# The last two of 32 experts in a one-core MoE block: order of the x1 loads, of one transpose, of the row scatters, and the branch behind them

## The chip, the core and the metric

The kernel runs on one core of one Trainium2 chip. The core has a matmul engine (TensorE, PE in the profile), a vector engine (VectorE, DVE), a scalar engine (ScalarE, ACT), a general-purpose engine (GpSimd, POOL) and a sequencer without arithmetic (SyncE, SP). Transfers between HBM and on-chip memory are issued from the queues of SP, ACT and POOL. The metric is the device time of one execution in microseconds (us), lower is better; 0.3% of it is 4.8 us.

## What is computed

One layer of a diffusion trunk: attention, gated linear attention and neighbourhood attention on 1024 tokens of width D = 1024, then a mixture of 32 experts in which every token goes to two experts, then a final RMS norm. Only the end of it matters here:

```python
f = hier_moe(h2.reshape(-1, D), w_rg, b_rg, w_re, b_re, w_up, w_down)
x = x + mod[:, 5] * f.reshape(B_, S, D)
...
return rms_norm(x, final_g)
```

An expert takes the rows of its tokens, multiplies them by `w_up` (1024x1024), applies `silu(g) * u` to the two halves, multiplies by `w_down` (512x1024), and its result, times the token's gate, is added to the token's row.

## The kernel before, in words

Each expert has one block of 128 slots (CAP); tokens beyond that go to overflow blocks. `gidx` holds the token of every slot. Experts 0 to 29 (ME = E - HOLD = 30 of them) run in the main loop: POOL gathers the rows, PE multiplies in three passes of rounded pieces, ACT scales the result by the gate, and POOL scatters it with an add into the HBM tensor YS (`y_scatter`, line 1882). The weights come as 128x1024 fp32 tiles (512 KB) through a ring of 34 tiles in SBUF (`ring`, `load_tile`, line 1909 for the issue).

The last two experts, 30 (ME) and 31 (E - 1), are **held**: they run in plain fp32 matmuls, and their results do not go through YS. Beside them the kernel finishes the output. For each of the 8 token tiles t, `pre(t)` (lines 2080 to 2088) multiplies YS's tile by the modulation row m5 on DVE (2082), adds it to the tile of x1, the stream before the experts (2083), writes the sum to the HBM tensor XP from ACT's queue (2084), and squares it on ACT with a row sum (2088). After all eight, `load_rows` (1968) gathers from XP the rows of the tokens that the held experts own, on POOL's queue. `norm` (2131) turns row sums into reciprocal square roots by a chain of eleven small DVE instructions; `scaled` (2135) multiplies a tile by it and by final_g on DVE; `store(t)` (2139) writes it to out from SP's queue. `result(e)` (2118, 2119) scales a held expert's result; it is added to the gathered rows, `cross` adds on PE and DVE the contribution of the first held expert to rows that both own, and `store_rows(i)` (2143) scatters the finished rows of expert ME + i over the output, from POOL's queue.

**What sets the order.** The held part stands in a manual schedule for PE, DVE, ACT and POOL: these run in the order of the program. SP is not in that list; its order is the scheduler's. The loads of the held part come from the list `wants`, one taken each time a tile of the ring comes free: eight x1 tiles (`load_x1`, line 1935), final_g, a tile without a load, the eight YS tiles (`load_y`, line 75 in the profile, a helper) and another tile without a load. A YS load waits for the last `y_scatter`, since YS is tracked in HBM. The first ten are taken in the main loop's last ten steps, the YS loads in `up(ME)`, one for each of its eight tiles. `after_all` makes a row scatter wait for every store and scatter to out before it, so the second row scatter waits for the first.

`up(e)` and `down(e)` are the held experts' two products on PE (line 1994), `hidden(e)` is silu on ACT and the product on DVE (1868, 1869), `turn_hidden(e)` transposes it on PE and copies it on ACT (1988, 1989). In the order before, `turn_hidden(E - 1)` and its ACT copy stand behind `pre(6)` and `pre(7)` and behind `down(ME)`.

Behind the held part stands a loop with as many turns as the register `again` says (line 2190 loads it on all five engines, 2191 is the loop). It is 1 when overflow blocks exist and 0 otherwise; with these inputs it is 0, and the loop's body, which handles overflow and writes the whole output again, is skipped.

Of the kernel before, what the change touches and what calls it, by code (L numbers as in the profile page):

```python
# [8 lines left out]
F32 = mybir.dt.float32  # L9
F32R = mybir.dt.float32r  # L10
I32 = mybir.dt.int32
# [7 lines left out]
D = 1024  # L19
# [46 lines left out]
def body(nc, tc, d, tap=None, upto=None):  # L66
# [7 lines left out]
    def dmab(t, src):  # L74
        nc.sync.dma_start(t, src)
# [1228 lines left out]
    class Til:  # L1304
# [5 lines left out]
        def small(self, name, shape, bufs=2):  # L1310
            return w2.tile([128] + shape, F32, name=name, bufs=bufs)
# [615 lines left out]
    def kept():  # L1927

        x2 = ring()
        rws.pop()  # L1930
        return x2

    def load_x1(t, eng):
        x2 = kept()
        eng.dma_start(x2, X1[t * 128:(t + 1) * 128, :])
        xts.append(x2)

    def small(name, shape):
        return e1.tile([128] + shape, F32, name=name)
# [2 lines left out]
    bs = small("bs", [NOV])  # L1942
    tk, dtk, both = small("tk", [HOLD]), small("dtk", [128]), small("both", [128])
    ones = small("ones", [128])

    def gate_of(e):
        return gxs[e % 6][:, e:e + 1]
# [11 lines left out]
    def held_both():  # L1959

        pt = pe.tile([128, 4, 128], F32, name="ept")
        nc.tensor.matmul(pt[:, 0, :], lhsT=ones, rhs=dtk, start=True, stop=True)
        V.tensor_scalar(both, pt[:, 0, :], tk[:, 0:1], None, op0=OP.is_equal)

    def load_rows(i):

# [5 lines left out]
    def load_y(t):  # L1972
        yts[t] = ring()
        dmab(yts[t], YS[t * 128:(t + 1) * 128, :])

    def load_fg():
        fgs.append(kept())
        dmab(fgs[0], bcast_rows(d["final_g"], D))

    ygs = []  # L1980
    wants = [lambda t=t: load_x1(t, nc.sync) for t in range(NT)] + [load_fg, lambda: ygs.append(kept())]
    wants += [lambda t=t: load_y(t) for t in range(NT)] + [lambda: ygs.append(kept())]

    def turn32(src, n, dst, g):
# [10 lines left out]

    yts, outs = {}, []

    def after_all(i_):

        for o_ in outs:  # L2000
            tc.add_manual_dep(i_.ins, o_.ins.name, mybir.DependencyInfo(mybir.DependencyClass.Sync, mybir.DependencyReason.DATA))

    with tc.manual_schedule(engines={ET.PE, ET.DVE, ET.Activation, ET.Pool}):
        e_gather(gU01[:, 0:1], xgs[0])
# [75 lines left out]
        def pre(t):  # L2080

            V.tensor_mul(yts[t], yts[t], m5)
            V.tensor_add(xts[t], xts[t], yts[t])
            nc.scalar.dma_start(XP[t * 128:(t + 1) * 128, :], xts[t])
            square(t)
# [4 lines left out]
        def up(e, ks):  # L2090
            if ks[0] == 0:
                pu[e] = pe.tile([128, D], F32, name="epu")
            for k in ks:
                mm32(pu[e], k, 8, loaded.pop(NM + 8 * (e - ME) + k), xs[e])
                fill()

        def hidden(e):
            sgs[e] = e_silu(pu[e])

        def turn_hidden(e):  # L2100
            if e == ME:
                a32[ME], a32[E - 1] = (a.bitcast(F32) for a in a_tiles())
            turn32(sgs[e], 4, a32[e], 0)

        def down(e):
            pys[e] = (pd.tile([128, D], F32, name="epy"), pe.tile([128, D], F32, name="epu"))[0] if e == ME else \
                pe.tile([128, D], F32, name="epu")
            for k in range(4):
                mm32(pys[e], k, 4, loaded.pop(NM + 8 * HOLD + 4 * (e - ME) + k), a32[e])
                fill()  # L2110

# [29 lines left out]
        def store_rows(i):  # L2141
            scaled(NT + i)
            i_ = nc.gpsimd.indirect_dma_start(out=d["out"], in_=xts[NT + i], in_offset=None,  # L2143
                                              out_offset=bass.IndirectOffsetOnAxis(ap=gU[:, ME + i:ME + i + 1], axis=0),
                                              bounds_check=T - 1, oob_is_err=False)
            after_all(i_)
            outs.append(i_)


        held_both()  # L2150
        up(ME, range(8))
        pre(0)
        pre(1)
# [5 lines left out]
        pre(4)  # L2159
        pre(5)  # L2160
        hidden(E - 1)
        pre(6)
        pre(7)
        for i in range(HOLD):
            load_rows(i)
        down(ME)
        turn_hidden(E - 1)
        down(E - 1)
        norm(0, 8)
        store(0)  # L2170
        store(1)
        store(2)
        result(ME)
        store(3)
        store(4)
        store(5)
        store(6)
        store(7)
        V.tensor_add(xts[NT], xts[NT], ygd[0])
        square(NT)  # L2180
        cross()
        result(E - 1)
        V.tensor_add(xts[NT + 1], xts[NT + 1], ygd[1])
        square(NT + 1)
        norm(NT, NT + HOLD)
        store_rows(0)
        store_rows(1)


    again = nc.values_load(novt[0:1, 1:2], min_val=0, max_val=1)  # L2190
    with tc.For_i(0, again, 1):
        for e in range(ME, E):
            y_scatter(ygs[e - ME], gU[:, e:e + 1])
        nov = nc.values_load(novt[0:1, 0:1], min_val=0, max_val=NOV)
        with tc.For_i(0, nov, 1) as i:
            ev = nc.values_load(bexp[0:1, ds(i, 1)], engines=[mybir.EngineType.SP], min_val=0, max_val=E - 1)
            gcol = e2.tile([128, 1], I32, name="gcol")
            gsel = e2.tile([128, 2, E], F32, name="gsel", bufs=1)
            g_ = e2.tile([128, 1], F32, name="g_")
            nc.vector.tensor_copy(gcol, gido[:, ds(i, 1)])  # L2200
            e_gather(gcol.bitcast(U32), xgs[0])
            gate_rows(gcol.bitcast(U32), gxs[0])
            nc.vector.tensor_copy(g_, bs[:, ds(i, 1)])
            nc.vector.tensor_scalar(gsel[:, 0, :], cio[:, :E], g_, None, op0=OP.is_equal)
            nc.vector.tensor_mul(gsel[:, 1, :], gsel[:, 0, :], gxs[0])
            nc.vector.tensor_reduce(g_, gsel[:, 1, :], axis=AX.X, op=OP.add)
            x, act = x_tiles(), a_tiles()
            for g in range(2):
                e_turn(xgs[0], 8, *x, g)
            pu_ = pe.tile([128, D], F32, name="epu")  # L2210
            for k, w in enumerate(e_load(d["w_up"][ds(ev, 1)].rearrange("o (k p) f -> p (o k) f", p=128), 8)):
                e_mm(pu_, k, 8, split(w), x)
            e_turn(e_silu(pu_), 4, *act, 0)
            py = pd.tile([128, D], F32, name="epy")
            for k, w in enumerate(e_load(d["w_down"][ds(ev, 1)].rearrange("o (k p) f -> p (o k) f", p=128), 4)):
                e_mm(py, k, 4, split(w), act)
            e_scatter(py, gcol.bitcast(U32), g_)
        for t in range(NT):
            xt, y0 = ring(), ring()
            dmab(xt, X1[t * 128:(t + 1) * 128, :])  # L2220
            dmab(y0, YS[t * 128:(t + 1) * 128, :])
            V.tensor_mul(y0, y0, m5)
            V.tensor_add(xt, xt, y0)
            nc.scalar.activation(y0, xt, AF.Square, accum_out=s3[:, t:t + 1])
            norm(t, t + 1)
            V.scalar_tensor_tensor(xt, xt, r3[:, 0, t:t + 1], fgs[0], op0=OP.mult, op1=OP.mult)
            after_all(nc.sync.dma_start(d["out"][t * 128:(t + 1) * 128, :], xt))
# [127 lines left out]
```

## Time and profile before

| | us |
|---|---|
| Median of three runs | 1604.22 (1602.19 to 1607.95) |
| The profiled execution, its own time | 1601.4 |
| Its span, first to last instruction | 1599.6 |

| Engine | Busy share of the span | Instructions |
|---|---|---|
| PE (matmul) | 91% | 8577 |
| DVE | 71% | 1882 |
| ACT | 60% | 1544 |
| POOL | 29% | 604 |

How to read it: the shares are means over the whole span, and the change lies in its last 95 us, from about 1505 us on. There the page's 40 slices (40 us each) say little; the views that count are the timeline by engine, the waits, and windows of a few us. A row of the timeline gives start, length, engine, line, operation, out<-in, count and, in brackets, the engine's idle time before it and what ended that. The transfers that an engine's queue issues stand under SPq, ACTq and POOL.

### The profile page before, as it was taken

The numbers are of one execution on the slowest core, as the hardware profiler recorded it, in microseconds if no ns is written. First come the engines' busy times: TensorE is split into PE (matmuls) and PEld (weight loads), VectorE is DVE, ScalarE is ACT, GpSimd is POOL, SyncE is SP. The second block draws the span as 40 slices with busy tenths as digits, with TensorE's granted clock in tenths as the row PEclk, the third lists the DMA queues.
The fourth block names the chain that finished last, engine by engine and source line by source line (L and its number), as shares of the span: only waits on it lengthen the run. The fifth ranks groups of instructions, "written<-read, shape, count | busy, mean of one in ns | idle before, by whom it ended". The sixth has DMA issues, their size and how long they took to land. (4 is left out here: it accounts for less than half of the span.)

```text
span 1599.6 us, 24460 instructions
## 1 busy us (share of the span) xinstructions
PE 1449.4 (91%) x8577; PEld 1183.7 (74%) x8577; DVE 1133.4 (71%) x1882; ACT 957.6 (60%) x1544; POOL 463.4 (29%) x604
## 2 busy tenths in 40 slices
PE   6899799889989997899999969999999999999972
PEld 3699577767767766789998857877877888788731
DVE  6612655894544455777777678999999999899755
ACT  3523554773534341677666437887888888888621
POOL 0001433222323211257887552221221122211101
PEclk8999899999988999899999979999999999999996
DMA  9533563014554389412222878999999999999963
GB/s 331 179 103 107 166 223 121 21 48 158 124 129 105 87 278 316 142 49 91 67 82 78 299 270 316 364 363 349 342 368 371 360 362 358 367 349 362 361 257 137
DMA packets 165119, 358.34 MB, mean 224 GB/s; under 512 B 29269, under 2 KB 85056, under 8 KB 164864
## 3 DMA queue, kind: packets, MB, share of 16 engines
q1 hardware_dynamic: 138656, 309.88, 54.6%
q0 software_dynamic: 22880, 36.80, 8.8%
q10 hardware_dynamic: 3456, 10.06, 1.6%
q8 instruction: 68, 1.11, 0.3%
q14 instruction: 59, 0.48, 0.1%
HBM read 319.87 MB, written 57.82 MB: 236 GB/s over the span
## 5 line engine op out<-in xcount | busy, mean ns | idle before, releaser
L1837 DVE TENSOR_TENSOR wlo<-wraw,whi 128x1024 fp32r<-128x1024 f32 x360 | 434.1, 1222 | 53.5 <-ACT whi L1836 48.1
L1836 ACT CAST whi<-wraw 128x1024 fp32r<-128x1024 f32 x360 | 372.5, 1050 | 99.7 <-PE epu L1864 59.0
L1862 PE MATMUL epu<-whi,xh 128*128 128x512 f32 x480 | 195.3, 407 | 2.2 <-ACT xh L1854 2.2
L1863 PE MATMUL epu<-wlo,xh 128*128 128x512 f32 x480 | 194.4, 405 | 0.4 <-DVE wlo L1837 0.4
L1864 PE MATMUL epu<-whi,xl 128*128 128x512 f32 x480 | 191.7, 399 | 0.6 <-DVE xl L1855 0.6
L1268 DVE TENSOR_REDUCE nm<-S 128x1 f32<-128x1280 f32 x64 | 94.9, 1489 | 51.6 <-PE S L1267 42.0
L1841 POOL DMA_INDIRECT xg<-H,gidx x30 | 31.9, 1064 | 342.0 <-PE ept L1852 341.5
L375 PE MATMUL pj<-wh,hh 128*128 128x256 f32 (+1 forms) x384 | 113.8, 296 | 3.1 <-ACT kbT L331 3.1
L1863 PEld LDWEIGHTS epu<-wlo,xh 128*128 128x128 f32 x480 | 91.4, 191 | 29.3 <-DVE wlo L1837 10.4
L377 PE MATMUL pj<-wh,hl 128*128 128x256 f32 (+1 forms) x384 | 112.4, 293 | 0.0
L376 PE MATMUL pj<-wl,hh 128*128 128x256 f32 (+1 forms) x384 | 112.4, 293 | 0.0
L1862 PEld LDWEIGHTS epu<-whi,xh 128*128 128x128 f32 x480 | 91.5, 191 | 22.7 <-ACT xh L1854 2.7
L1864 PEld LDWEIGHTS epu<-whi,xl 128*128 128x128 f32 x480 | 91.2, 190 | 21.8 <-DVE xl L1855 1.3
L1862 PE MATMUL epy<-whi,ah 128*128 128x512 f32 x240 | 100.9, 421 | 2.4 <-ACT y L1888 2.4
L364 PE MATMUL pj<-hh,wh 128*128 128x512 f32 (+1 forms) x240 | 99.8, 416 | 0.0
L1273 ACT ACTIVATE p<-S,nm 128x1280 f32<-128x1280 f32 x64 | 84.6, 1331 | 21.8 <-DMA x1t<-w_out 16.4
L1864 PE MATMUL epy<-whi,al 128*128 128x512 f32 x240 | 95.6, 398 | 0.0
L1863 PE MATMUL epy<-wlo,ah 128*128 128x512 f32 x240 | 95.1, 396 | 0.0
L366 PE MATMUL pj<-hh,wl 128*128 128x512 f32 (+1 forms) x240 | 92.1, 384 | 0.0
L365 PE MATMUL pj<-hl,wh 128*128 128x512 f32 (+1 forms) x240 | 91.9, 383 | 0.0
L1266 PE MATMUL S<-ak,aq 128*128 128x512 f32 (+1 forms) x192 | 75.3, 392 | 12.1 <-ACT p L1273 11.3
L1288 ACT COPY eT<-apt 128x512 f32<-128x512 f32 (+1 forms) x96 | 46.4, 515 | 63.8 <-PE apt L1287 61.9
(485 smaller groups left out, 3476.3 us busy)
## 6 DMA issues: line engine op xcount, KB each, us to landing
wraw<-w_up SPq DMA_DIRECT2D x254, 512.0 KB
wraw<-w_down SPq DMA_DIRECT2D x127, 512.0 KB
wm<-w_mod SPq DMA_DIRECT2D x32, 512.0 KB
raw<-w_in SPq DMA_DIRECT2D x22, 512.0 KB
wm<-w_mod SPq DMA_DIRECT2D x32, 256.0 KB
aq<-QS SPq DMA_DIRECT2D x64, 128.0 KB
ak<-KS SPq DMA_DIRECT2D x8, 640.0 KB
xn<-x SPq DMA_DIRECT2D x8, 512.0 KB
```

Of the source, the lines that this page charges most:

```text
L364: nc.tensor.matmul(ps[:, :n], lhsT=a, rhs=x, start=(k == 0), stop=False)
L365: nc.tensor.matmul(ps[:, :n], lhsT=a, rhs=y, start=False, stop=False)
L366: nc.tensor.matmul(ps[:, :n], lhsT=b, rhs=x, start=False, stop=(k == 7))
L375: nc.tensor.matmul(ps[:, :n], lhsT=a, rhs=wh[:, k, :], start=(k == 0), stop=False)
L376: nc.tensor.matmul(ps[:, :n], lhsT=a, rhs=wl[:, k, :], start=False, stop=False)
L377: nc.tensor.matmul(ps[:, :n], lhsT=b, rhs=wh[:, k, :], start=False, stop=(k == 7))
L1268: V.tensor_reduce(u.nm[:, m:m + 1], sv, axis=AX.X, op=OP.max, negate=True)
L1836: nc.scalar.copy(hi, raw)
L1837: nc.vector.tensor_sub(lo, raw, hi.bitcast(F32))
L1862: nc.tensor.matmul(ps[:, cs], lhsT=ah[:, k, :], rhs=hi[:, cs], start=(k == 0), stop=False)
L1863: nc.tensor.matmul(ps[:, cs], lhsT=ah[:, k, :], rhs=lo[:, cs], start=False, stop=False)
L1864: nc.tensor.matmul(ps[:, cs], lhsT=al[:, k, :], rhs=hi[:, cs], start=False, stop=(k == nk - 1))
```

## The change

- The x1 loads of tiles 2 to 7 are no longer issued when their tile of the ring comes free (`room_x1` only keeps the tile) but in `load_y`: x1 tile t + 2 behind YS tile t.
- `turn_hidden(E - 1)` moves from behind `pre(7)` and `down(ME)` to the middle of `down(ME)`, and `down(ME)` and this transpose move ahead of `pre(6)` and `pre(7)`.
- `held_both` gets five small DVE instructions that build `own`: for a token that both held experts own, the first expert's row index is pushed out of bounds, so that its row is written by the second scatter alone. The scatters use `own`, and each waits for the eight stores only, not for the other scatter.
- In the last part, `result(ME)`, the addition and the square of the first row tile stand after four stores, not eight; the norm of the two row tiles becomes two norms; and the first row scatter is issued before `cross` and `result(E - 1)`.
- `again` is loaded into the engines' registers at the start of the held part, and the last loop becomes a conditional on it.

```diff
@@ -1930,10 +1930,13 @@
         rws.pop()
         return x2
 
-    def load_x1(t, eng):
-        x2 = kept()
-        eng.dma_start(x2, X1[t * 128:(t + 1) * 128, :])
-        xts.append(x2)
+    def load_x1(t):
+        nc.sync.dma_start(xts[t], X1[t * 128:(t + 1) * 128, :])
+
+    def room_x1(t):
+        xts.append(kept())
+        if t < 2:
+            load_x1(t)
 
     def small(name, shape):
         return e1.tile([128] + shape, F32, name=name)
@@ -1942,6 +1945,8 @@
     bs = small("bs", [NOV])
     tk, dtk, both = small("tk", [HOLD]), small("dtk", [128]), small("both", [128])
     ones = small("ones", [128])
+    again2 = small("again2", [1])
+    own = e1.tile([128, HOLD], I32, name="own")
 
     def gate_of(e):
         return gxs[e % 6][:, e:e + 1]
@@ -1961,6 +1966,11 @@
         pt = pe.tile([128, 4, 128], F32, name="ept")
         nc.tensor.matmul(pt[:, 0, :], lhsT=ones, rhs=dtk, start=True, stop=True)
         V.tensor_scalar(both, pt[:, 0, :], tk[:, 0:1], None, op0=OP.is_equal)
+        V.tensor_reduce(again2, both, axis=AX.X, op=OP.max)
+        V.tensor_scalar(again2, again2, 8192.0, None, op0=OP.mult)
+        V.tensor_add(again2, again2, tk[:, 0:1])
+        V.tensor_copy(own[:, 0:1], again2)
+        V.tensor_copy(own[:, 1:2], gidx[:, E - 1:E])
 
     def load_rows(i):
 
@@ -1972,13 +1982,15 @@
     def load_y(t):
         yts[t] = ring()
         dmab(yts[t], YS[t * 128:(t + 1) * 128, :])
+        if t + 2 < NT:
+            load_x1(t + 2)
 
     def load_fg():
         fgs.append(kept())
         dmab(fgs[0], bcast_rows(d["final_g"], D))
 
     ygs = []
-    wants = [lambda t=t: load_x1(t, nc.sync) for t in range(NT)] + [load_fg, lambda: ygs.append(kept())]
+    wants = [lambda t=t: room_x1(t) for t in range(NT)] + [load_fg, lambda: ygs.append(kept())]
     wants += [lambda t=t: load_y(t) for t in range(NT)] + [lambda: ygs.append(kept())]
 
     def turn32(src, n, dst, g):
@@ -1995,10 +2007,12 @@
 
     yts, outs = {}, []
 
+    FULL = mybir.DependencyInfo(mybir.DependencyClass.Sync, mybir.DependencyReason.DATA)
+
     def after_all(i_):
 
         for o_ in outs:
-            tc.add_manual_dep(i_.ins, o_.ins.name, mybir.DependencyInfo(mybir.DependencyClass.Sync, mybir.DependencyReason.DATA))
+            tc.add_manual_dep(i_.ins, o_.ins.name, FULL)
 
     with tc.manual_schedule(engines={ET.PE, ET.DVE, ET.Activation, ET.Pool}):
         e_gather(gU01[:, 0:1], xgs[0])
@@ -2102,10 +2116,10 @@
                 a32[ME], a32[E - 1] = (a.bitcast(F32) for a in a_tiles())
             turn32(sgs[e], 4, a32[e], 0)
 
-        def down(e):
-            pys[e] = (pd.tile([128, D], F32, name="epy"), pe.tile([128, D], F32, name="epu"))[0] if e == ME else \
-                pe.tile([128, D], F32, name="epu")
-            for k in range(4):
+        def down(e, ks=range(4)):
+            if ks[0] == 0:
+                pys[e] = pd.tile([128, D], F32, name="epy") if e == ME else pe.tile([128, D], F32, name="epu")
+            for k in ks:
                 mm32(pys[e], k, 4, loaded.pop(NM + 8 * HOLD + 4 * (e - ME) + k), a32[e])
                 fill()
 
@@ -2141,13 +2155,15 @@
         def store_rows(i):
             scaled(NT + i)
             i_ = nc.gpsimd.indirect_dma_start(out=d["out"], in_=xts[NT + i], in_offset=None,
-                                              out_offset=bass.IndirectOffsetOnAxis(ap=gU[:, ME + i:ME + i + 1], axis=0),
+                                              out_offset=bass.IndirectOffsetOnAxis(ap=own.bitcast(U32)[:, i:i + 1], axis=0),
                                               bounds_check=T - 1, oob_is_err=False)
-            after_all(i_)
+            for o_ in outs[:NT]:
+                tc.add_manual_dep(i_.ins, o_.ins.name, FULL)
             outs.append(i_)
 
 
         held_both()
+        again = nc.values_load(novt[0:1, 1:2], min_val=0, max_val=1)
         up(ME, range(8))
         pre(0)
         pre(1)
@@ -2159,36 +2175,34 @@
         pre(4)
         pre(5)
         hidden(E - 1)
+        down(ME, range(2))
+        turn_hidden(E - 1)
+        down(ME, range(2, 4))
         pre(6)
         pre(7)
         for i in range(HOLD):
             load_rows(i)
-        down(ME)
-        turn_hidden(E - 1)
         down(E - 1)
-        norm(0, 8)
-        store(0)
-        store(1)
-        store(2)
+        norm(0, NT)
+        for t in range(4):
+            store(t)
         result(ME)
-        store(3)
-        store(4)
-        store(5)
-        store(6)
-        store(7)
         V.tensor_add(xts[NT], xts[NT], ygd[0])
         square(NT)
+        for t in range(4, 7):
+            store(t)
+        norm(NT, NT + 1)
+        store(7)
+        store_rows(0)
         cross()
         result(E - 1)
         V.tensor_add(xts[NT + 1], xts[NT + 1], ygd[1])
         square(NT + 1)
-        norm(NT, NT + HOLD)
-        store_rows(0)
+        norm(NT + 1, NT + 2)
         store_rows(1)
 
 
-    again = nc.values_load(novt[0:1, 1:2], min_val=0, max_val=1)
-    with tc.For_i(0, again, 1):
+    with tc.If(again > 0):
         for e in range(ME, E):
             y_scatter(ygs[e - ME], gU[:, e:e + 1])
         nov = nc.values_load(novt[0:1, 0:1], min_val=0, max_val=NOV)
```

## Rows read from the trace of the kernel before

**Rows 1.** Chain of waits in order of time: start us, us, what.

```profile
1582.51 1.80 DMA out<-wraw,gidx
1584.31 3.49 issue
...
1588.39 0.62 POOL out L2143
```

**Rows 2.** Timeline of DVE and PE in the held part.

```profile
1532.98 1.23 DVE L2082 TENSOR_TENSOR wraw<-wraw,m 128x1024 f32<-128x1024 f32 x1 [15.83 <-DMA wraw<-YS]
...
1552.32 0.69 DVE L1869 TENSOR_TENSOR sg<-sg,epu 128x512 f32<-128x512 f32 x1 [2.07 <-ACT sg L1868]
...
1556.58 1.22 DVE L2083 TENSOR_TENSOR wraw<-wraw 128x1024 f32<-128x1024 f32 x1
...
1559.88 10.13 PE L1994 MATMUL epu<-wraw,al 128*128 128x512 f32 x16 [6.16 <-ACT al L1989]
...
1561.62 3.68 DVE L2135 SCALAR_TENSOR_TENSOR wraw<-wraw,r 128x1024 f32<-128x1024 f32 x3
...
1572.51 1.22 DVE L2179 TENSOR_TENSOR wraw<-wraw,wlo 128x1024 f32<-128x1024 f32 x1
...
1578.78 0.17 DVE L2131 TENSOR_SCALAR s<-s 128x2 f32<-128x2 f32 x1 [1.27 <-ACTq L2191]
...
1580.94 2.48 DVE L2135 SCALAR_TENSOR_TENSOR wraw<-wraw,r 128x1024 f32<-128x1024 f32 x2
```

**Rows 3.** Timeline of SP's queue from 1505 us on.

```profile
1506.48 11.61 SPq L1935 DMA_DIRECT2D wraw<-X  x8
1519.05 0.33 SPq L75 DMA_DIRECT2D wraw<-final_g  x1
1526.26 8.25 SPq L75 DMA_DIRECT2D wraw<-YS  x8
1562.93 10.02 SPq L2139 DMA_DIRECT2D out<-wraw  x8
```

**Rows 4.** Timeline of POOL from 1500 us on.

```profile
1517.17 1.55 POOL L1882 DMA_INDIRECT YS<-y,gidx  x1 [8.33 <-DVE both L1963]
1561.56 1.07 POOL L1968 DMA_INDIRECT wraw<-XP,gidx  x1 [42.84 <-issue]
...
1582.51 1.80 POOL L2143 DMA_INDIRECT out<-wraw,gidx  x1 [17.53 <-DVE wraw L2135]
1588.02 0.99 POOL L2143 DMA_INDIRECT out<-wraw,gidx  x1 [3.71 <-issue]
```

**Rows 5.** Lines 1882, 1968 and 2143, one row each: us from issue to landing.

```profile
DMA to landing us min/median/max: 6.7/9.1/10.5
...
DMA to landing us min/median/max: 4.8/6.6/8.3
...
DMA to landing us min/median/max: 3.2/4.0/4.7
```

**Rows 6.** Windows: length, busy us per engine (instructions), PEclk, DMA share, GB/s.

```profile
1522.00:1528.00 6.00, 6.00 (x16) 2.65 (x15) 0.00 (x0) 0.00 (x0) 0.00 (x0) 1.00 0.60 184
1528.00:1541.00 13.00, 13.00 (x32) 5.79 (x31) 5.82 (x6) 2.79 (x5) 0.00 (x0) 1.00 1.01 383
1559.00:1560.20 1.20, 0.32 (x1) 0.32 (x2) 0.68 (x4) 0.83 (x3) 0.00 (x0) 0.50 0.76 311
1560.20:1563.00 2.80, 2.80 (x4) 1.19 (x4) 2.56 (x9) 0.00 (x0) 1.14 (x2) 0.50 0.00 0
```

**Rows 7.** Lines 2190, 2191 and 2351: duration ns min/median/max, first and last start.

```profile
L2190 SPq TENSOR_LOAD <-novt x1: 480/480/480, 1534.6 to 1534.6; - x1
...
L2190 PEldq TENSOR_LOAD <-novt x1: 1507/1507/1507, 1566.9 to 1566.9; - x1
...
L2191 POOLq INC_SWDGE_SEM  x1: 1750/1750/1750, 1588.9 to 1588.9; - x1
...
L2351 POOLq DRAIN  x3: 46/103/6404, 1592.3 to 1599.3; - x3
```

## Prediction, made before the changed kernel was run

> **What bounds it now.** Read the chain of waits first, since it tells which end counts [rows 1]: the last pieces are the transfer of a row scatter into out, 3.5 us in which POOL waits, and the other row scatter. So the end is set by POOL's second scatter. POOL's timeline [rows 4] says why it is so late: the first is issued at 1582.51, the second at 1588.02, though both were scaled by 1583.42 (1580.94 + 2.48) [rows 2]. The gap is the wait for the first to land, between 3.2 and 4.7 us [rows 5].
>
> Next, DVE's timeline [rows 2]. From 1532.98 to 1583.42 DVE hardly rests; before that it idles 15.83 us, and what ends the idling is the first YS tile. SP's timeline shows the cause of that [rows 3]: the eight x1 loads go out from 1506.48 on, final_g at 1519.05, and the YS loads only at 1526.26, since they wait for the last scatter into YS, issued at 1517.17 [rows 4]. The first YS tile then needs another 6.7 us, behind x1 tiles still under way. The windows [rows 6] show the transfer engines at 0.60 of their time from 1522 to 1528, and full, at 383 GB/s, from 1528 to 1541. So the tail has three limits in a row: the scatter into YS with what queues around it, then DVE's list, then POOL's two scatters.
>
> PE is not among them: the last held product starts at 1559.88 after a 6.16 us wait and takes 10.13 us at the low clock (granted 0.50, that is 1.2 GHz [rows 6]), and DVE reaches its result only after 1572.51 [rows 2].
>
> **Part by part**, against the profiled execution (span 1599.6, own time 1601.4, which is 2.8 below the median 1604.22; I take the difference off the median).
>
> *x1 loads behind the YS loads.* Six transfers leave the queue ahead of the scatter and final_g. Scatters into YS land 6.7 to 10.5 us after issue, median 9.1 [rows 5], nearly all beside weight loads. I take 6.7, since the queues would then be nearly free: landing at 1517.17 + 6.7 = 1523.9 instead of about 1526.2. The bounds are 4.7, the worst of the scatters into out, which do not add, and 9.1. The Trainium skill (DMA: Bandwidth & Descriptors, Anatomy of one DMA) gives a transfer issued by GpSimd about 2.0 us plus its bytes over 436 GB/s, some 3.2 us for 512 KB as an estimate; the scatters into out agree (3.2 to 4.7), those into YS do not (6.7 and up), and by that price the forecast would be 3.5 us lower.
>
> How long a lone load takes is bounded by an XP write: pre(7)'s addition ends at 1557.80 and its write, issued behind it, is moved by 1560.2, after which no byte moves [rows 2, 6], so 2.4 us or less; the upper bound is the 6.7 us seen. I take 2.9, near the free one: the first YS tile is there at 1526.8 and DVE starts 6 us earlier.
>
> It cannot keep those 6 us. A tile of 524 kB at 383 GB/s [rows 6] takes 1.37 us. The queue is now y0, x1(2), y1, x1(3), ..., and y5 is its eleventh load; four XP writes will have come between. So y5 is there 10 + 4 = 14 transfers after y0: 1526.8 + 19.2 = 1546.0. pre(5) takes 1.23 + 1.22, then DVE waits 2.07 for silu and multiplies for 0.69 (as at 1552.32), then come pre(6) and pre(7), 4.9 us [rows 2]: 1546.0 + 2.45 + 2.8 + 4.9 = 1556.1, against 1557.80. y7, 19 transfers after y0, is there at 1552.8, in time. **Gain 1.7 us**; the rest of the 6 has gone into the transfer engines.
>
> *Last transpose moved forward.* Its ACT copy no longer stands behind two squares, so PE starts the last product about 6 us sooner, probably at the high clock. Nothing late waits for it: cost and gain 0, covered by DVE's list. Its place in `down(ME)` makes PE wait for DVE's product in mid-way; `result(ME)` wants that output some 8 us later.
>
> *Reordered end.* From 1557.80 to 1583.42 DVE needed 25.6 us; the same instructions remain, and one chain for the norm is added, 1580.94 - 1578.78 = 2.16 us. The gathered rows are wanted sooner. Before, DVE reached their addition 3.82 us (to 1561.62) plus 10.89 us after pre(7); with four stores of 1.23 us fewer ahead it is 9.8 us. The first gather is issued 3.76 us after pre(7) and lands 4.8 to 8.3 us later [rows 2, 4, 5], so 8.6 to 12.1: a wait of 0 to 2.3 us. I take 0.5, since only a few stores compete by then. Together 25.6 + 2.2 + 0.5 = 28.3: the last row is scaled at 1584.4.
>
> *Independent scatters.* The second scatter is issued about 0.3 us after its row is scaled (the first was ready at 1582.18 and began at 1582.51): 1584.7 instead of 1588.02, **gain 3.3 us for all parts so far**. The first goes out some 7 us before it and waits only for eight stores. Landing took 3.2 us for one scatter and 4.7 for the other; I take 4.0, so 0.8 is lost.
>
> *Building own.* Five small DVE instructions of 0.2 to 0.4 us at about 1517, within DVE's 15.83 us of idling: 0. Were that cover gone, some 1.5 us.
>
> *Register loads moved, conditional for loop.* A load took 0.48 us on SP and 1.51 on PE [rows 7]. On PE it now stands ahead of `up(ME)` and shifts both up products by 1.5 us; behind it all PE work of the held part waits, but silu of expert 31 waits for the square of pre(5) anyway. On SP it stands near the YS loads, which wait for the scatter then: 0. Whether the conditional closes faster than a loop without a turn the trace cannot show. POOL's 1.75 us for its counter ran while the scatter was landing, and could come after it; the 6.4 us drain of POOL behind it all [rows 7] could at best go. Bounds: 6.4 us less, 1.75 more. I take 0, as POOL has the same transfers to settle.
>
> Sum: -3.3 + 0.8 = -2.5 us, a span of 1597.1 and a median of about **1601.7 us**. Its own range is 1598 to 1605: landing in 4.7 gives 2 more, in 9.1 takes 2.4; the gather takes up to 1.8; a tile at 1.3 us gives 1.
>
> **Rivals.**
>
> 1. *The order does not come out as written.* SP is left to the scheduler, and the trace has it out of program order: the register load of line 2190, written behind everything, runs on SP at 1534.6 [rows 7], ahead of the eight stores from 1562.93 on [rows 3]. x1 tiles wait for nothing by then, YS tiles do, so x1 may be put first again. Against it: in the same trace the register load, ready long before, was not put ahead of the YS loads. Then DVE starts at 1532.98 as before, pre(7) ends at 1557.80, the second scatter goes at 1557.80 + 28.3 + 0.3 = 1586.4, gain 1.6 less 0.8: **1603.4**.
>
> 2. *The queues are freer than I think*: the scatter lands in 4.7 us and the XP writes give way to the loads. y0 is there at 1524.8, DVE is the limit (24.8 us from 1532.98 to 1557.80), pre(7) ends at 1549.6, and without a wait for the gather the second scatter goes at 1549.6 + 27.8 + 0.3 = 1577.7, 10.3 sooner: **1594.7**. Against it: full engines from 1528 to 1541. The skill's 3.2 us would make it 1.5 us less.
>
> 3. *Slower: the moved loads collide.* The place is the wait of pre(5) for y5; the price six more transfers, 8.2 us, in the stretch that is full already. If the scatter lands no sooner and y0 again takes 6.7 us, it is there at 1532.9 as before, y5 at 1552.1, pre(7) ends at 1562.2, and with a gather wait of 2.3 the second scatter goes at 1592.6: 4.6 later, 5.4 with the landing: **1609.6**. It decides from the point at which y5 lands after 1548.5: then pre(7) ends after 1558.6, which uses up what the scatters gain. For it: 0.60 of the engines' time from 1522 to 1528, left unused by x1 then.
>
> **Numbers.** Forecast 0.50, rival 1 0.23, rival 2 0.13, rival 3 0.14. The range 1595.5 to 1607.5 leaves out about half of rivals 2 and 3. About 0.3% (4.8 us) is what a measurement of this kernel can tell from no change. Faster by more, under 1599.4: three in ten of the forecast, a little of rival 1, all but a little of rival 2, with the unknown of the closing: 0.33. Slower, over 1609.0: over half of rival 3, little else: 0.09. The rest, 0.58, is within.
>
> **What would show it.** Right: on SP the x1 loads stand between YS loads; the scatter into YS lands in under 7 us; DVE's idling ends at about 1527, but DVE waits again, for YS tiles, between pre(3) and pre(5); the two scatters are issued some 7 us apart, without a wait between them; the last one at about 1584.7; POOL's drain of 6.4 us is still there. Wrong: eight x1 loads in one run ahead of final_g (rival 1); no second wait of DVE (rival 2); pre(7) ending after 1558.6 (rival 3); or a drain of another length.

## The result and the profile after

The changed kernel takes 1596.02 us (median of 14 runs, 1585.59 to 1601.54), the kernel before beside it 1604.59 us (14 runs, 1595.54 to 1612.22): a ratio of 0.9941, 95% interval 0.9918 to 0.9964. It is faster by 0.6%. A second measurement on another occasion gave 0.9956 (0.9934 to 0.9979). Two executions in this study, of 4853.16 and 2037.62 us, are left out of every ratio as slow ones.

The profiled execution of the changed kernel took 1598.41 us, with a span of 1596.6 us. That is only 3.0 us less than the span before. The reason is in work that the change leaves alone: the last scatter into YS, the end of the main loop, was issued at 1517.17 before and at 1521.03 after. In the profiled executions of all kernels of this study it lies anywhere between 1509.15 and 1523.53. So a single span says little about an edit of a few us. What can be compared is the **tail**, from the issue of this last scatter (called T0 from here on) to the end of the span: 1599.6 - 1517.17 = 82.4 us before, 1596.6 - 1521.03 = 75.6 us after, 6.9 us less. A repeat of both kernels gave 82.8 and 75.7. These 6.9 of 1604 us are 0.43%, a ratio of 0.9957, which both intervals contain.

The chain of waits of the changed kernel (start us, us, what), to be read against [rows 1]:

```profile
1581.35 1.61 DMA out<-wraw,own
1582.95 3.84 issue
1586.79 0.05 POOLq L2205
...
1587.03 1.00 POOL out L2157
```

POOLq is POOL's sequencer, which hands out the instructions and waits on semaphores. The chain looks like the old one: a row scatter's transfer, an issue gap of 3.8 us, the other scatter. This reading is wrong here, as DVE's timeline shows (columns as in [rows 2]):

```profile
1532.23 1.22 DVE L2096 TENSOR_TENSOR wraw<-wraw,m 128x1024 f32<-128x1024 f32 x1 [10.27 <-DMA wraw<-YS]
...
1535.69 1.23 DVE L2096 TENSOR_TENSOR wraw<-wraw,m 128x1024 f32<-128x1024 f32 x1 [0.98 <-DMA wraw<-YS]
...
1546.45 1.22 DVE L2096 TENSOR_TENSOR wraw<-wraw,m 128x1024 f32<-128x1024 f32 x1 [0.68 <-DMA wraw<-YS]
...
1557.83 1.23 DVE L2097 TENSOR_TENSOR wraw<-wraw 128x1024 f32<-128x1024 f32 x1
...
1569.10 1.23 DVE L2190 TENSOR_TENSOR wraw<-wraw,wlo 128x1024 f32<-128x1024 f32 x1
...
1575.82 2.47 DVE L2149 SCALAR_TENSOR_TENSOR wraw<-wraw,r 128x1024 f32<-128x1024 f32 x2
...
1585.46 1.28 DVE L2149 SCALAR_TENSOR_TENSOR wraw<-wraw,r 128x1024 f32<-128x1024 f32 x1
```

The last row tile is scaled at 1585.46 + 1.28 = 1586.74, and the second scatter goes at 1587.03, 0.29 us behind it. DVE's list now sets the end of this stretch. The two short waits, 0.98 and 0.68 us for YS tiles, are new.

POOL's timeline (for [rows 4]):

```profile
1521.03 1.55 POOL L1882 DMA_INDIRECT YS<-y,gidx  x1 [8.34 <-DVE both L1968]
1562.89 1.07 POOL L1978 DMA_INDIRECT wraw<-XP,gidx  x1 [40.32 <-issue]
...
1581.35 1.61 POOL L2157 DMA_INDIRECT out<-wraw,own  x1 [15.11 <-DVE wlo L2132]
1587.03 1.00 POOL L2157 DMA_INDIRECT out<-wraw,own  x1 [4.08 <-DVEq L2205]
```

SP's timeline (for [rows 3]) shows that the order came out as written, two x1 tiles ahead and the others between the YS tiles:

```profile
1510.97 1.60 SPq L1934 DMA_DIRECT2D wraw<-X  x2
1513.51 0.33 SPq L75 DMA_DIRECT2D wraw<-final_g  x1
1528.45 0.33 SPq L75 DMA_DIRECT2D wraw<-YS  x1
1528.82 0.42 SPq L1934 DMA_DIRECT2D wraw<-X  x1
1529.35 0.38 SPq L75 DMA_DIRECT2D wraw<-YS  x1
1529.77 0.43 SPq L1934 DMA_DIRECT2D wraw<-X  x1
```

The windows (columns as in [rows 6]) show the price and the use of the emptier stretch. From 1522 to 1528 little but the scatter into YS is under way; of the 0.38 MB moved, 0.11 MB are what is left of the earlier loads:

```profile
1522.00:1528.00 6.00, 6.00 (x16) 2.65 (x15) 0.00 (x0) 0.00 (x0) 0.57 (x1) 1.00 0.36 64
1528.00:1541.00 13.00, 13.00 (x32) 5.77 (x31) 5.60 (x6) 2.78 (x5) 0.00 (x0) 1.00 0.89 310
1541.00:1547.00 6.00, 6.00 (x17) 2.65 (x16) 5.25 (x5) 0.00 (x0) 0.00 (x0) 1.00 1.02 417
```

Last, the lines of the conditional and of the closing on POOL, and of the register load (duration ns min/median/max, first and last start, for [rows 7]):

```profile
L2205 POOLq EVENT_SEMAPHORE  x3: 17/43/43, 1587.3 to 1587.5; - x3
...
L2205 POOLq INC_SWDGE_SEM  x1: 1759/1759/1759, 1587.6 to 1587.6; - x1
...
L2365 POOLq DRAIN  x3: 46/103/6402, 1589.4 to 1596.3; - x3
...
L2166 PEldq TENSOR_LOAD <-novt x1: 494/494/494, 1516.0 to 1516.0; - x1
```

The 6.4 us drain is unchanged. It begins as soon as the 1.76 us for POOL's counter is over (1587.6 + 1.76), 2.33 us behind the scatter's issue; before it began at 1592.35 - 1588.02 = 4.33 us behind it [rows 4, 7].

**Where the 6.9 us come from.** The tail is cut into three stretches at two marks, the end of the last y + x1 unit (pre(7), DVE line 2083 before, 2097 after) and the issue of the second row scatter. All times in us, from the timelines:

| | before | after | gain |
|---|---|---|---|
| T0 to the end of pre(7) | 1557.80 - 1517.17 = 40.63 | 1559.06 - 1521.03 = 38.03 | 2.60 |
| pre(7) to the second scatter | 1588.02 - 1557.80 = 30.22 | 1587.03 - 1559.06 = 27.97 | 2.25 |
| second scatter to the end | 1599.6 - 1588.02 = 11.58 | 1596.6 - 1587.03 = 9.57 | 2.01 |

### The profile page after: what moved, and what is told of

Its sections match the earlier page's. It is cut to its first block, busy times and chain, and to the rows that moved or that the text cites. A ratio compares the mean times of both kernels' runs of the same rounds, so it can differ in the third digit from the quotient of the medians.

```text
span 1596.6 us, 24416 instructions
## 1 busy us (share of the span) xinstructions
PE 1448.2 (91%) x8577; PEld 1182.3 (74%) x8577; DVE 1136.5 (71%) x1898; ACT 957.7 (60%) x1544; POOL 462.2 (29%) x604
## 3 DMA queue, kind: packets, MB, share of 16 engines
q8 instruction: 68, 1.11, 0.3%
## 5 line engine op out<-in xcount | busy, mean ns | idle before, releaser
L1268 DVE TENSOR_REDUCE nm<-S 128x1 f32<-128x1280 f32 x64 | 94.9, 1489 | 51.1 <-PE S L1267 41.4
```

What stands on the lines that cost most here:

```text
L1268: V.tensor_reduce(u.nm[:, m:m + 1], sv, axis=AX.X, op=OP.max, negate=True)
```

## The experiments

Each kernel below is read by these three stretches of its profiled execution. Single device times are not used, for those of one kernel vary by 6 us or more either way; where a ratio is given, it comes from 11 or 12 runs.

**Both kernels again.** No edit. They show how far the stretches of the same kernel agree.

> The kernel before once more, for the spread of one look. Measured is the tail, from the issue of the last scatter into YS to the end of the span; it was 82.4 us before (1517.17 to 1599.6) and is 75.6 us after the change (1521.03 to 1596.6). Theory A (the whole gain lies in the tail, and the start of the tail merely scatters from run to run): tail 82.4 within 1 us, and its start anywhere from 1512 to 1524. Rival B (the change also shifted the work ahead of the tail): the start is near 1517.2 again, and one of the changed kernel near 1521.

> The changed kernel once more. Theory A: tail 75.6 within 1 us, start of the tail anywhere from 1512 to 1524, and over the rounds 0.3 to 0.6% faster than before, since 6.9 us is 0.43%. Rival B: start near 1521 again, or a ratio beyond 0.8%, which the tail could not give.

Measured: before 41.0 + 30.3 + 11.6 = 82.8 us, after 38.2 + 28.0 + 9.6 = 75.7 us, ratio 0.9956 (0.9934 to 0.9979). The second and third stretch repeat within 0.1 us, and a difference of 0.2 us in them can be read. The first repeats within 0.4 here, but it varies more than that: the seven profiles of this study with two x1 loads early have 37.2 to 39.1 us (mean 38.1), the four with all eight early 40.3 to 41.0 (mean 40.6). In one profile, less than about 2 us in the first stretch, and so in the tail, can't be laid to an edit.

**The loop back in place of the conditional**, in the changed kernel; the registers are still loaded early.

```diff
-    with tc.If(again > 0):
+    with tc.For_i(0, again, 1):
```

> The changed kernel with the loop in place of the conditional, the register still loaded early. Theory A: the loop's closing waits for the landing of the last scatter before POOL's drain of 6.4 us may start, the conditional's does not; from the issue of the last row scatter to the start of the drain 4.3 us as before the change, not 2.3, and a tail of 77.6. Rival C (the 2 us came from the register load, which no longer stands between scatter and drain): 2.3 us to the drain and a tail of 75.6.

POOL's lines of the loop and of the end, in that kernel:

```profile
L2205 POOLq EVENT_SEMAPHORE  x15: 17/43/1111, 1581.6 to 1586.2; - x15
...
L2365 POOLq DRAIN  x3: 46/103/6404, 1586.4 to 1593.4; - x3
```

The second scatter went at 1581.70, so the drain begins 4.72 us behind it, not 2.33, and the third stretch is 11.96 us, not 9.57. The other two are as in the changed kernel (37.2, 28.0). One of the 15 waits takes 1.11 us and ends when the scatter has landed, 3.6 us behind its issue: the loop, even without a turn, asks at its close for what was under way, and goes through a row of semaphores. The conditional's 3 waits take at most 0.04 us each. So the gain at the end is the conditional's, and not the early register load's. The trace of the kernel before has the same row, and of it the part behind POOL's counter, which ends at 1588.89 + 1.75 = 1590.64 [rows 7]:

```profile
L2191 POOLq EVENT_SEMAPHORE  x15: 17/43/43, 1588.6 to 1592.1; - x15
...
L2191 POOLq EVENT_SEMAPHORE  x12: 43/43/43, 1591.2 to 1592.1; - x12
```

No wait there is longer than 43 ns, so before the change POOL did not wait for the landing: the scatter landed 3.2 us behind its issue [rows 5], at 1591.2, just when POOL asked for it. The 2.0 us are the loop's own steps. From the counter's end to the drain at 1592.35 pass 1.71 us, with two branches, 12 semaphore instructions 0.09 us apart and 0.44 us without a row; with the conditional it is 0.03 us. The other 0.33 us lie ahead of the counter, which starts 0.87 us behind the scatter's issue before and 0.54 us behind it with the conditional.

**The conditional alone**, in the kernel before, with the register load moved forward as in the change.

```diff
         held_both()
+        again = nc.values_load(novt[0:1, 1:2], min_val=0, max_val=1)
...
-    again = nc.values_load(novt[0:1, 1:2], min_val=0, max_val=1)
-    with tc.For_i(0, again, 1):
+    with tc.If(again > 0):
```

> The kernel before with nothing but the conditional and the early register load. Theory A: last row scatter to drain 2.3 us in place of 4.3, tail 80.4. Rival C, where the register load alone did it: the same here, so this run says only whether 2 us are got without the other parts. If they depend on the other parts: 82.4.

POOL's timeline and the drain in that kernel:

```profile
1580.04 1.80 POOL L2143 DMA_INDIRECT out<-wraw,gidx  x1 [17.53 <-DVE wraw L2135]
1584.86 0.99 POOL L2143 DMA_INDIRECT out<-wraw,gidx  x1 [3.02 <-issue]
```

```profile
L2351 POOLq DRAIN  x3: 46/103/6402, 1587.2 to 1594.2; - x3
```

The drain begins 2.34 us behind the scatter: the 2.0 us are there without the rest of the change. And the second scatter goes 29.5 us behind pre(7), not 30.2: its idle gap is 3.02 instead of 3.71 us [rows 4]. POOL's register load, which stood near this gap, is not the reason. The sequencer's wait for the first scatter's landing, before and here, is:

```profile
L2143 POOLq EVENT_SEMAPHORE  x1: 4912/4912/4912, 1582.3 to 1582.3; - x1
...
L2143 POOLq EVENT_SEMAPHORE  x1: 4231/4231/4231, 1579.9 to 1579.9; - x1
```

The second scatter goes 0.75 us behind the end of this wait in both, with the load and without it. The wait is 0.68 us shorter because the first scatter landed 4.0 us behind its issue and not 4.7 [rows 5]; the repeat of the kernel before has 4.8, and why it is slower there stays open. The tail is 79.4 us, 3 less than before.

**All x1 loads early again**, in the changed kernel.

```diff
-        if t < 2:
+        if t < 8:
             load_x1(t)
...
-        if t + 2 < NT:
-            load_x1(t + 2)
```

> The changed kernel with all eight x1 loads issued as before, ahead of final_g and the YS loads. Theory A: the first YS tile is there again some 15.8 us after the issue of the last scatter into YS (11.2 with the change), pre(7) ends 40.6 us after it (38.0), and the tail is 2.6 us longer: 78.2. Rival D (the order of the loads only moves the same transfers about): pre(7) ends at 38.0 and the tail is 75.6, within 0.7.

SP's timeline and the start of DVE's in that kernel:

```profile
1506.18 11.61 SPq L1934 DMA_DIRECT2D wraw<-X  x8
1518.75 0.33 SPq L75 DMA_DIRECT2D wraw<-final_g  x1
1525.86 8.39 SPq L75 DMA_DIRECT2D wraw<-YS  x8
```

```profile
1532.70 1.23 DVE L2094 TENSOR_TENSOR wraw<-wraw,m 128x1024 f32<-128x1024 f32 x1 [16.22 <-DMA wraw<-YS]
```

With T0 at 1516.97, the first YS load goes 8.9 us behind the scatter and DVE starts 15.7 us behind it, as before; pre(7) ends at 40.6. So the whole first gain, 2.5 us, is that of the order of the x1 loads; the means above, 40.6 and 38.1, give the same. It has two parts: the scatter lands 7.4 us behind its issue in the changed kernel instead of 8.9, and the first YS tile comes 3.8 us behind its load's issue instead of 6.8. The second is the firmer one: 3.7 to 3.8 in all seven profiles with two loads early. Of DVE's 4.5 us earlier start 2.0 are given back before pre(7) ends, 0.98 + 0.68 = 1.66 of them to its two waits for YS tiles.

**The two scatters chained again**, in the changed kernel: the second waits for the first by a dependency, as before.

```diff
-            for o_ in outs[:NT]:
-                tc.add_manual_dep(i_.ins, o_.ins.name, FULL)
+            after_all(i_)
             outs.append(i_)
```

> The changed kernel with the second row scatter waiting for the first again. Theory A: nothing is lost. With the change the first is issued at 1581.35 and has landed at about 1585.2, before the second is ready at 1586.8; what counts is that the first goes out early. Tail 75.6, within 0.7. Rival E (the independence itself is what pays, as the prediction had it): the second is issued 3 us later, tail 78.6.

POOL's timeline in that kernel:

```profile
1584.78 1.76 POOL L2157 DMA_INDIRECT out<-wraw,own  x1 [14.97 <-DVE wlo L2132]
1590.61 1.00 POOL L2157 DMA_INDIRECT out<-wraw,own  x1 [4.07 <-DVEq L2204]
```

Nothing is lost: the second scatter goes 27.97 us behind pre(7), to the hundredth as in the changed kernel, and the gap ahead of it is the same 4.1 us. Either the chain costs nothing because the first scatter has landed by the time that the second row is ready, or it was never gone. In the changed kernel itself POOL's sequencer waits 4.04 us behind the first scatter:

```profile
L2157 POOLq EVENT_SEMAPHORE  x1: 4044/4044/4044, 1581.2 to 1581.2; - x1
```

The next two kernels tell what this wait is.

**One norm for both row tiles, both scatters at the end**, otherwise the changed kernel; the end as before, with `own`.

```diff
-        for t in range(4, 7):
+        for t in range(4, 8):
             store(t)
-        norm(NT, NT + 1)
-        store(7)
-        store_rows(0)
...
-        norm(NT + 1, NT + 2)
+        norm(NT, NT + HOLD)
+        store_rows(0)
         store_rows(1)
```

> The changed kernel with one norm chain for both row tiles and both scatters at the end, as in the order before, but the scatters still independent. Theory A: DVE's list is 2.0 us shorter, both scatters are ready within 1.3 us of each other, POOL issues them back to back (1.6 us for the first), so the second is issued 1 to 1.5 us earlier than with the change, counted from the end of pre(7): 26.5 to 27.0 us in place of 27.97, tail about 74.4. Rival F (two scatters at once disturb each other, or the first one's early issue matters): landing 2 us longer, tail 76 or more.

Line 2157 on POOL in that kernel, its sequencer's wait and the transfers' landing:

```profile
L2157 POOLq EVENT_SEMAPHORE  x1: 4190/4190/4190, 1577.2 to 1577.2; - x1
...
DMA to landing us min/median/max: 3.2/3.6/4.0
```

This missed: the second scatter was to follow the first by its issue alone and went 29.62 us behind pre(7). POOL waited 4.19 us between the two, until the first had landed. The scatters are **not independent in the changed kernel**: leaving out the hand-made dependency left one that is derived from both writing out. Its 29.62 us also split the second gain: 1.65 of the 2.25 us are lost with the first scatter back beside the second, and 0.6 stay, as the first landed in 4.0 us here and in 4.7 before. Measured over 12 runs this kernel is at 0.9961 of before (0.9944 to 0.9978).

**The same with the scatters really free**: the derived dependency is declared void, which `own` allows, as the two scatters write different rows.

```diff
             for o_ in outs[:NT]:
                 tc.add_manual_dep(i_.ins, o_.ins.name, FULL)
+            for o_ in outs[NT:]:
+                tc.declare_no_dep(i_.ins, o_.ins.name, reason="...")
             outs.append(i_)
```

> Both held rows' norm together again (as before) and, in addition, the second row scatter is declared free of the first. Theory A (POOL's 4 us wait ahead of the second scatter, for the first one's landing, is a dependency left standing by the dependency tracker; with it gone two scatters at the end cost only their own issue): the second scatter is issued 1.6 to 1.9 us behind the first, 26.5 to 27.3 us after the end of the last y+x1 unit (29.62 with the wait, 27.97 in the changed kernel), and the time from the last scatter into YS to the end of the program is 73.7 to 74.6 us (76.86 and 75.57). Theory B (the wait belongs to the queue: a second scatter isn't issued on it until the first has landed, dependency or not): the wait of 4 us stays and the second scatter is again at 29.4 to 29.9. Theory C (the dependency goes, but two scatters close together land later): second scatter at 26.5 to 27.3, and its landing 5 us or more behind its issue, so that the tail stays at 75 to 77.

Line 2157 on POOL, POOL's timeline and the drain in that kernel:

```profile
L2157 POOLq EVENT_SEMAPHORE  x1: 17/17/17, 1579.7 to 1579.7; - x1
```

```profile
1579.87 1.80 POOL L2157 DMA_INDIRECT out<-wraw,own  x1 [17.65 <-DVE wraw L2149]
1581.98 1.00 POOL L2157 DMA_INDIRECT out<-wraw,own  x1 [0.30 <-issue]
```

```profile
L2365 POOLq DRAIN  x3: 46/103/6402, 1583.4 to 1590.4; - x3
```

The wait of 4.19 us is gone (17 ns). The second scatter goes 2.11 us behind the first (up to 1.9 was expected) and 26.93 us behind pre(7). The drain begins 1.4 us behind the second scatter and is again 6.4 us, so that the tail is 74.2 us, inside what the first theory gave. The queue itself holds nothing back. The second and third stretch together are 2.0 us shorter than in the changed kernel; the tail is 1.4 us shorter, since the first stretch came out 0.6 us longer, within its spread. In device time the two can't be told apart: 0.9939 of before (0.9914 to 0.9964, 11 runs).

**The last transpose back behind pre(7)**, and the first held product with it, in the changed kernel.

```diff
-        down(ME, range(2))
-        turn_hidden(E - 1)
-        down(ME, range(2, 4))
         pre(6)
         pre(7)
         for i in range(HOLD):
             load_rows(i)
+        down(ME)
+        turn_hidden(E - 1)
         down(E - 1)
```

> The changed kernel with the last transpose and the first held product at their old place behind pre(7). Theory A: PE starts the last product some 3 us later and at the low clock, but DVE wants it only about 20 us after pre(7); tail 75.6, within 0.7. Rival G (the earlier product matters, through result(ME) or cross): result(ME) now comes after four stores, about 9 us after pre(7), and would wait for PE: tail 76.5 to 78.

PE's timeline in that kernel:

```profile
1552.03 9.99 PE L2006 MATMUL epu<-wraw,al 128*128 128x512 f32 x16 [5.31 <-ACT al L2001]
```

The same product in the changed kernel:

```profile
1558.25 7.03 PE L2006 MATMUL epu<-wraw,al 128*128 128x512 f32 x16
```

With the transpose moved, the product follows without an idle gap and takes 7.03 us at a granted clock of 1.00 (2.4 GHz); with it back, PE idles 5.31 us and the product takes 9.99 us at a mean of 0.71, its first 5 us at 0.50 (1.2 GHz). Nothing comes of it: with the transpose back the second scatter goes 27.97 us behind pre(7) and the tail is 75.4 us. The step is off the path.

**Four x1 loads early instead of two**, in the changed kernel.

```diff
-        if t < 2:
+        if t < 4:
             load_x1(t)
...
-        if t + 2 < NT:
-            load_x1(t + 2)
+        if t + 4 < NT:
+            load_x1(t + 4)
```

> The changed kernel with four x1 loads ahead of the first y load instead of two. Theory A (the DMA engines are nearly idle between the landing of the early loads and that of the last scatter into YS, so two more loads fit in there and are then missing from the y loads' queue): the y+x1 units' waits for loads fall from 1.1 to 1.7 us to below 0.6, the y0 load is still issued 6.8 to 8.2 us after the last scatter into YS, the last unit ends 36.3 to 37.3 us after that scatter (37.2 to 38.2 in the changed kernel), and the tail is 74.3 to 75.2 us. Theory B (any further load ahead lies in the scatter's way, as all eight do): y0 is issued after 8.5 us or more and the last unit ends at 38.3 or later; tail 76 or more.

DVE's waits for YS tiles in that kernel:

```profile
1533.04 1.23 DVE L2096 TENSOR_TENSOR wraw<-wraw,m 128x1024 f32<-128x1024 f32 x1 [11.46 <-DMA wraw<-YS]
...
1536.02 1.22 DVE L2096 TENSOR_TENSOR wraw<-wraw,m 128x1024 f32<-128x1024 f32 x1 [0.49 <-DMA wraw<-YS]
...
1546.88 1.23 DVE L2096 TENSOR_TENSOR wraw<-wraw,m 128x1024 f32<-128x1024 f32 x1 [0.80 <-DMA wraw<-YS]
```

The waits stay (0.49 + 0.80 = 1.3 us), the first YS load goes 8.7 us behind the scatter, pre(7) ends at 38.7, and the tail is 76.2 us. The first theory fails; every sign of the second came, but 38.7 also lies among the seven profiles with two loads early, so no loss is shown either. The scatter's landing can't be laid to the loads from this, since it took 8.7 us in the free-scatter kernel too, which has two loads early; with two it lies between 6.8 and 8.7 us in the seven profiles, with four at 8.7 and 8.8, with eight at 8.9 to 9.1 in four profiles. With eight early loads the scatter lands later than in any profile with two; between two and four these runs don't decide.

**Four early, one norm, free scatters** together.

> Both together: four early x1 loads, one norm for both held rows, scatters free of each other. Theory A of both: the gains add, last unit at 36.3 to 37.3 and the second scatter 26.5 to 27.3 us after it, tail 72.6 to 73.6 us, that is some 2.5 us less than in the changed kernel, and about 9 less than before. Rival: what the earlier units gain is lost to waits for the TensorE results of the held pairs (which have less cover now), so that the stretch from the last unit's end to the second scatter grows by what the units gained: tail 73.9 or more.

Measured: pre(7) at 39.2 us, the second scatter 26.95 us behind it, tail 74.8 us; the ratio is 0.9964 (0.9941 to 0.9986). The sum of the first theory didn't come, yet not for the rival's reason: the end keeps its whole gain, no wait for PE's results appears, and the four early loads show no gain. The kernel with the free scatters and two early loads has the shortest tail of all, by 0.6 us, which is within the spread of the first stretch.

## Why the prediction was wrong

The forecast was a change of -2.5 us, within 0.3%; measured are 0.6% and 0.4% in the two timings and 6.9 us in the tail. The range held the median by 0.5 us, which is luck as the sum missed the closing. Each step, from T0, so that the shift of the main loop is out of it:

| | forecast | measured |
|---|---|---|
| YS scatter lands | 6.7 | 7.4 |
| first YS tile, from its load's issue | 2.9 | 3.8 |
| DVE starts | 9.6 | 11.2 |
| waits of DVE for YS tiles | between pre(3) and pre(5) | 0.98 at pre(1), 0.68 at pre(4) |
| pre(7) ends | 1556.1 - 1517.17 = 38.9 | 38.0 |
| DVE's list, pre(7) to the last scaling | 28.3 | 27.7 |
| second scatter issued | 1584.7 - 1517.17 = 67.5 | 66.0 |
| second scatter to the end | 11.6 + 0.8 = 12.4 | 9.6 |

**The step that failed is the closing.** The prediction put "I take 0, as POOL has the same transfers to settle", and charged 0.8 us more for a later landing. The runs showed 2.0 us less, and no trace of the landing. Its wrong idea was that the end waits for the transfers, so that their settling is all there is to count. Before, POOL found the last scatter landed when the loop asked for it, and the 2.0 us were the loop's own closing steps, 1.7 us of them between the counter and the drain; only with the loop in the changed kernel did POOL wait there for the landing, 1.11 us. The drain doesn't wait for it either. Its 6.40 us are the same whether it begins 1.1 us after the landing, as before (1592.35 against 1588.02 + 3.2 [rows 5]), or, as in the free-scatter kernel, 1.4 us behind the last scatter's issue. In the changed kernel the bytes go on for about a us after the drain's start at 1589.36, as three windows show:

```profile
1587.03:1589.36 2.33, 0.00 (x0) 0.00 (x0) 0.00 (x0) 0.00 (x0) 1.00 (x1) 0.50 0.20 74
1589.36:1590.50 1.14, 0.00 (x0) 0.00 (x0) 0.00 (x0) 0.00 (x0) 0.00 (x0) 0.50 0.20 79
1590.50:1596.60 6.10, 0.00 (x0) 0.00 (x0) 0.00 (x0) 0.00 (x0) 0.00 (x0) 0.50 0.01 1
```

The two mistakes together, 2.8 us, are most of the 4.4 us that the forecast was short by. The rest is sizes: pre(7) 0.9 and DVE's list 0.6.

**x1 loads** (gain 1.7 forecast, 2.6 measured): the mechanism was right, an earlier start of which the transfer engines take a part back, and the size was off in three terms that partly cancel. The scatter took 7.4 us although the engines moved 64 GB/s meanwhile, so "nearly free queues" did not bring the 6.7. The first tile took 3.8, not 2.9. But the tiles behind it came quicker than 1.37 us each: y4, eight loads and three or four XP writes behind y0, is there 1546.45 - 1532.23 = 14.2 us after it, 1.2 to 1.3 us a transfer, in agreement with 417 GB/s from 1541 to 1547. So the expected wait for y5 shrank to 1.7 us in all.

The prediction counted 512 KB for a scatter, the size of the tile. Fewer bytes move, since slots without a token write nothing: 0.27 MB for the one into YS (window 1522 to 1528) and 0.26 MB for the first into out (1581.3 to 1585.3; queue: packets, MB, share of the 16 engines):

```profile
q0 software_dynamic: 143, 0.27, 31.2%
...
q0 software_dynamic: 144, 0.26, 16.7%
```

The Trainium skill (DMA: Bandwidth & Descriptors, Anatomy of one DMA) has about 2.0 us plus bytes over 436 GB/s for a transfer issued by GpSimd, which gives an estimate of 2.6 us for these bytes. Neither kind agrees: the row scatters into out took 3.2 to 4.8 us over all profiles, and the scatter that adds into YS took 7.4 us with little beside it. The agreement that the prediction saw came of the 512 KB.

**Reordered end** (27.7 against 28.3): the second norm's chain is there, 1575.82 - 1573.83 = 2.0 us for 2.16, and the addition of the gathered rows at 1569.10 begins without a wait, where 0.5 was taken.

**Independent scatters**: the forecast of the second scatter's place was right, 0.3 us behind DVE's last scaling, but not by the reason given. Independence was not reached, as the one-norm kernel shows; what works is that the first scatter goes 5.7 us ahead of the second, which covers its landing of about 4 us, so the remaining wait ends 1.5 us before the second row is ready. "Without a wait between them" was wrong, harmlessly so.

**Last transpose, own, register load**: 0 forecast for each, and no run speaks against it. The earlier product gained nothing, as the run with the transpose back shows. `own` and the early load were not undone by themselves; DVE still idles 10.27 us behind the instructions of `own`, and PE's register load took 0.49 us and not 1.51.

**Rivals.** 1 fell: SP's order is as written. 2 fell: the scatter did not land in 4.7 us, and DVE still waits. 3 fell: pre(7) ends at 38.0 us from T0, where this rival decides from 1558.6 - 1517.17 = 41.4 on. The bound for the closing, "6.4 us less", held the truth, but it was given no weight: between -6.4 and +1.75 the value nearest to no change was taken for want of a row, and the one place that could have told, the 15 semaphore waits of the loop's line between 1588.5 and the drain, was not put into the sum. The rows at hand held 1.7 us of it: the counter is over at 1590.6 and the drain begins at 1592.3 [rows 7], while the last scatter has landed at 1591.2 [rows 5].

## What to carry to other kernels

Read what stands between the last issue and the end as work of its own: here the closing of a loop without a turn took POOL 2 us longer than that of a conditional, by its own steps and not by a transfer. Look at how long each semaphore instruction took before you call it a wait. A dependency that you leave out by hand can still be there by the tracker: look for the wait in the sequencer's rows, and test it with the cover taken away. Before comparing spans of a few us, find a mark behind which the kernels differ and measure from there, since the stretch ahead of it moved by 14 us between profiles; then cut at further marks, since the first stretch behind it still varied by 2 us.

## What the runs showed of the hardware

- POOL's closing drain took 6.40 us in the profile of every kernel, whether or not transfers were still moving when it began.
- From the last scatter's issue to the drain POOL took 4.33 us with the loop and 2.33 us with the conditional; in the kernel before, none of the loop's 15 semaphore instructions on POOL took more than 43 ns.
- A scatter of 0.27 MB that adds into HBM took 7.4 us to land with the engines at 0.36 of their time and 64 GB/s (6.8 to 8.7 us in the seven profiles with two loads early), against 3.2 to 4.8 us for the scatters of 0.25 to 0.30 MB into out.
- The same register load took 1.51 us on PE when it stood near the end [rows 7] and 0.49 us near 1516 us; on SP 0.48 and 0.53.
